# RWKV-7 mixer, r and v phases: decay factors loaded one row tile ahead, each tile's stores issued behind the next tile's products

## The chip, the cores and the metric

The kernel runs on one core of one Trainium2 chip. The metric is the device time of one execution of the whole program in microseconds; the time given is the median of several runs.

The engines are named as in the profile: PE is TensorE (matmuls; PEld is its weight load), DVE is VectorE, ACT is ScalarE, POOL is GpSimd and SP is SyncE, which issues most of the DMAs, one after the other in the order of its queue.

## The reference, cut to what matters

The model is a trunk of two layers over 1024 positions of width 1024. Layer 0 mixes tokens with a Griffin RG-LRU block, layer 1 with RWKV-7; each layer also has a cross-attention into a memory and a squared-ReLU MLP. The change touches the RWKV-7 mixer alone:

```python
def rwkv7_mixer(x, mu, w_rkv, w0, w1, w2, a0, a1, a2, g1, g2, k_k, k_a, r_k, gn_g, gn_b, w_o):
    xx = x_prev - x                       # x_prev: x shifted by one position
    r = (x + xx * mu[0]) @ w_rkv[0]
    k = (x + xx * mu[2]) @ w_rkv[1]
    v = (x + xx * mu[3]) @ w_rkv[2]
    ...                                   # decay, a, g, kk from small products
    def step(state, inp):                 # 1024 steps for each of 16 heads of 64
        r_t, w_t, k_t, v_t, a_t, b_t = inp
        sa = jnp.einsum('bhij,bhj->bhi', state, a_t)
        state = (state * w_t[:, :, None, :] + sa[..., None] * b_t[:, :, None, :]
                 + v_t[..., None] * k_t[:, :, None, :])
        y_t = jnp.einsum('bhij,bhj->bhi', state, r_t)
        return state, y_t
    _, ys = lax.scan(step, state0, seq_inputs)
    ...                                   # group norm of y, bonus term of r, k and v
    return (out * g) @ w_o
```

All values are float32. The scan is done in chunks of time, by matmuls; a small triangular system is solved in each chunk.

## The kernel before, in words

A float32 product is made of three matmuls: each operand is split into a high part, cast on ACT (L233), and a low part, subtracted on DVE (L234), and `mm3` issues high by high, high by low and low by high (L318, L319, L320). The three large products of the mixer are made one after another, k, r and v. Each is worked off in eight row tiles f of 128 channels by 1024 positions, in turns: for r the turns are [0,1], [2], [3], [4], [5] and [6,7], for v they begin with [0,1] and go on with single tiles. `fphase` makes the matmuls of one turn, 48 groups of three for each tile into one PSUM buffer `p` of 128 by 1024, of which there are two, so a tile's matmuls need the buffer that the tile two before it has left. The weights of a tile are loaded at L249 and split by L233 and L234.

In the r phase a tile is finished by `evac_r`: `early` has loaded the tile of decay factors from Pd (L1530), DVE multiplies it by the product (L1534), and SP stores the result to MVd (L1535). In the v phase `early` loads the tile of r from MVd and another from STd (L1622, L1624). `evac_v` copies the product (ACT, L1574), multiplies r by its partner (DVE, L1581) and splits this product, transposes v on TensorE (L1591), copies it to `vk` (ACT, L1592) and, behind every odd tile, stores `vk` to sv0 (L1598) and Vd (L1602). Then it makes the bonus term and the gate: matmuls against ones (L1609), DVE L1610, the three matmuls of the gate, ACT L1613 and DVE L1614, and four stores to G1d and G2d (L1617).

Beside these runs work for the triangular systems, in pieces between the turns. `gram` makes the matrices and stores them (L1426, L1427). A solve of 31 pairs of steps runs on DVE or POOL (L1447, L1449). A `merge` of solved blocks makes small matmuls (L1486, L1493) with ACT copies behind each (L1488, L1496); its operands are loaded at L1472, L1473 and L1474, and the merged block is stored at L1500. L1553 copies small tables into `db`. Near the end of the v phase the first loads of the scan are issued (L1645, L1648, L1659), and the scan itself begins with more (L1672, L1676).

What sets the order: the code is written as a list of calls, and the framework's scheduler, which simulates times of its own, puts the instructions of each engine into the one order in which that engine works them off (L1930). `self.behind()` and `self.line()` pin some of it. `depth` and `ahead` tell how many tiles ahead the weights are taken and fetched. SP waits at the head of its queue for what its next DMA needs, a DMA's source or a free buffer, and every DMA behind it waits with it.

The functions that the diff touches:

Of the kernel before, what the change touches and what calls it, by code (L numbers as in the profile page):

```python
# [1281 lines left out]
def rwkv(self, X, xt, lw_wa, lw_g, post, mid):  # L1282
    nc, I = self.nc, self.I
    mm = nc.tensor.matmul
    hgd = self.dram([128, 1024])
    Vd = self.dram([1024, 2, 512])
# [245 lines left out]
    def evac_r(f, p):  # L1532
        r = ld.pop(f)
        nc.vector.tensor_mul(r, r, p)  # L1534
        nc.sync.dma_start(MVd[:, f, 1, :], r)  # L1535

    for i, fs in enumerate([[0, 1], [2], [3], [4], [5], [6, 7]]):
        for f in fs:
            early(f)
        if i == 5:  # L1540
            self.later.append(lambda: rwkv_make_mix(self, X, 3, 0, xv[0], range(3)))
        if i in (1, 2):
            sums(5 + i)
        self.depth, self.ahead = DA if i != 4 else (DA[0], DA[1] + 1)
        self.fphase(I["b_w_rkv"][0, 0], fs, xr, evac_r, spread=i == 0)
        if i == 0:
            prep_rest(7)
        if i in (1, 2):
            gram(5 + i)
        if i == 3:  # L1550
            for par in range(2):
                for h in range(2):
                    nc.sync.dma_start(self.db.rearrange("p (f a t) -> p f a t", a=2, t=8)[hr[h], :, par],  # L1553
                                      self.d2.rearrange("p (f h t) -> p f h t", h=2, t=8)[hr[par], :, h])
        aside(len(TURNS) + i)
# [12 lines left out]
    vk = []  # L1568
    sv0 = [self.unit() for _ in range(2)]

    def evac_v(f, p):
# [15 lines left out]
        for e in range(2):  # L1587
            pt = self.bank()
            for i in range(4):
                tt = e * 4 + i  # L1590
                mm(pt[:, i * 128:i * 128 + 128], vt[:, tt * 128:tt * 128 + 128], self.center, start=True, stop=True)  # L1591
            nc.scalar.copy(vk[e].rearrange("p (t h g i) -> p t h g i", h=2, g=2, i=64)[:, :, :, f % 2, :],  # L1592
                           pt.rearrange("p (t h i) -> p t h i", h=2, i=64))
            if f % 2 and e == 0:

                for d in range(2):
                    for h in range(2):
                        nc.sync.dma_start(sv0[d][hr[1 - h], h * 512 + (f - 1) * 64:h * 512 + (f + 1) * 64],  # L1598
                                          vk[0].rearrange("p (t h i) -> p t h i", h=2, i=128)[hr[d], 0, h, :])
            if f % 2:  # L1600
                for h in range(2):
                    nc.sync.dma_start(Vd[e * 512:e * 512 + 512, h, (f - 1) * 64:(f + 1) * 64].rearrange("(t p) i -> p t i", p=128),  # L1602
                                      vk[e].rearrange("p (t h i) -> p t h i", h=2, i=128)[:, :, h, :])
        g1 = self.unit()
        for e in range(2):
            s = slice(e * 512, e * 512 + 512)
# [5 lines left out]
            self.mm3(gp, (g2[0][:, cs], g2[1][:, cs]), (hg[0][:, s], hg[1][:, s]), True, True)  # L1612
            nc.scalar.activation(g1[:, s], gp, AF.Copy, scale=self.col("gn_g", f))  # L1613
            nc.vector.scalar_tensor_tensor(vt[:, s], vt[:, s], self.col("gn_b", f), gp, ALU.add, ALU.mult)  # L1614
        for src, dst in ((g1, G1d), (vt, G2d)):
            for h in range(2):
                nc.sync.dma_start(dst[(f % 2) * 64:(f % 2) * 64 + 64, (f // 2) * 2 + h, :], src[h * 64:h * 64 + 64, :])  # L1617

    def early(f):
        cs = slice(f * 128, f * 128 + 128)  # L1620
# [142 lines left out]
    for i, fs in enumerate(turns):  # L1763
        for f in turns[i + 1] if i < 6 else []:
            early(f)
        if fs[-1] >= 5:
            self.depth, self.ahead = min(2, 7 - fs[-1]), 0
        self.fphase(I["b_w_rkv"][0, 2], fs, xv, evac_v, spread=i == 0)
        aside(len(TURNS) + 6 + i)
        if fs[-1] == LD:  # L1770
            with self.behind():
                load(0)
        if fs[-1] == 6:
            load_solved(0)
            load(1)
    with self.behind():
        load_solved(1)
    for c in range(2):
# [156 lines left out]
```

## Time and profile before

| what | value |
| --- | --- |
| runs shown | 2838.39, 2846.89, 2841.48 us; median 2841.48 |
| profiled execution | 2839.18 us, span 2837.5 us |
| mean granted TensorE clock | 0.995 |
| PE busy | 2765.8 us, 97% of the span |
| DVE, ACT, POOL busy | 1867.1, 1422.8, 907.3 us |
| r and v phases | about 1488 to 1730 us of the span |
| SP's waits for DVE L1534 at L1535, 1545 to 1700 us | 25.0 us in 4 waits, longest 12.9 |
| SP's waits for ACT L1613 at L1617, same stretch | 18.3 us in 3 waits, longest 9.8 |

A row of a timeline has the start, the duration of all its instructions together, the engine, the line and operation, output and input names, shapes and the number of instructions; in brackets stands how long the engine had been idle before it and what ended that. A row of windows gives the stretch, busy times by engine, the granted clock of TensorE, the busy share of the DMA engines and GB/s. Rows of SP are DMA issues: what they last is the time of issue, not that of the transfer.

### The profile page before, as it was taken

The page shows a single profiled execution, that of the slowest core. Times are in us where ns is not written, and L with a number is a line of the kernel's source. Part 1 is how long each engine was busy: PE and PEld are TensorE (multiplying, and loading weights), DVE is VectorE, ACT ScalarE, POOL GpSimd, SP SyncE. Part 2 cuts the span into 40 slices and gives each one's busy share as a digit, 9 for nine tenths or more (in the row PEclk, how much of TensorE's full clock was granted, in tenths as well). Part 3 has the DMA queues.
Part 4 walks back from the last instruction along what each step waited for, and adds up shares of the span by engine and source line. Part 5 has one row for each costly group of instructions (what it writes and reads, how often), then busy time and mean ns, then how long its engine had stood idle before and what let it go on. Part 6 is the DMA issues. An engine that isn't in the chain of part 4 may idle for free.

```text
span 2837.5 us, 42691 instructions
## 1 busy us (share of the span) xinstructions
PE 2765.8 (97%) x16955; PEld 2310.6 (81%) x16955; DVE 1867.1 (66%) x2017; ACT 1422.8 (50%) x2194; POOL 907.3 (32%) x962
## 2 busy tenths in 40 slices
PE   7999999999999999999999999999999999999998
PEld 6888788888888888887777777888888888888887
DVE  5477557658454577898685834785675755467778
ACT  6456355545545553346672534664563644555333
POOL 2000113014666510013088223853203376640002
PEclk9999999999999999999999999999999999999999
DMA  8212352323454554423558799962222355474453
GB/s 266 75 45 75 104 171 79 103 84 104 148 164 153 206 205 156 155 98 126 170 146 228 218 247 244 238 158 96 79 93 89 99 167 162 141 244 168 149 177 120
DMA packets 383912, 421.92 MB, mean 149 GB/s; under 512 B 91504, under 2 KB 294496, under 8 KB 383712
## 3 DMA queue, kind: packets, MB, share of 16 engines
q1 hardware_dynamic: 371680, 379.19, 44.1%
q0 software_dynamic: 11568, 39.41, 3.8%
q8 instruction: 133, 2.18, 0.3%
q14 instruction: 67, 0.55, 0.1%
q10 hardware_dynamic: 464, 0.59, 0.1%
HBM read 283.79 MB, written 134.74 MB: 148 GB/s over the span
## 4 chain that ended last, share of the span: by engine, by line
PE 44%; DVE 4%; ACT 2%; DMA 2%; issue 1%; SPq 1%; POOL 1%; DVEq 0%; POOLq 0%; ACTq 0%
PE q L318 8%; PE q L319 8%; PE q L320 8%; PE p L318 4%; PE p L320 4%; PE p L319 4%; PE q L1700 1%; DVE u L234 1%; DMA u<-d 1%; PE q L1811 1%; PE q L1823 1%; PE q L1348 1%; PE q L1724 1%; DMA u<-in_b_w_rkv 1%; PE q L1836 0%
## 5 line engine op out<-in xcount | busy, mean ns | idle before, releaser
L234 DVE TENSOR_TENSOR u<-u,u 128x1024 fp32r<-128x1024 f32 (+1 forms) x602 | 813.0, 1381 | 346.4 <-ACT u L233 331.1
L233 ACT CAST u<-u 128x1024 fp32r<-128x1024 f32 (+1 forms) x602 | 591.8, 1020 | 446.6 <-DVE u L1077 224.6
L318 PE MATMUL q<-u,u 128*128 128x512 f32 (+1 forms) x1952 | 744.7, 383 | 4.4 <-DVE u L370 2.1
L319 PE MATMUL q<-u,u 128*128 128x512 f32 (+1 forms) x1952 | 745.0, 382 | 0.0
L320 PE MATMUL q<-u,u 128*128 128x512 f32 (+1 forms) x1952 | 739.7, 382 | 0.0
L318 PE MATMUL p<-u,u 128*128 128x512 f32 (+1 forms) x1472 | 553.5, 378 | 14.5 <-ACT u L233 6.4
L319 PE MATMUL p<-u,u 128*128 128x512 f32 (+1 forms) x1472 | 552.5, 375 | 3.7 <-DVE u L234 3.5
L320 PE MATMUL p<-u,u 128*128 128x512 f32 (+1 forms) x1472 | 551.2, 375 | 4.0 <-DVE u L234 3.9
L328 POOL TENSOR_SCALAR s<-s 128x1 f32<-128x1 f32 x97 | 43.7, 451 | 1252.0 <-ACT u L326 1250.1
L318 PEld LDWEIGHTS q<-u,u 128*128 128x128 f32 x1952 | 366.9, 188 | 77.3 <-ACT u L361 1.5
L320 PEld LDWEIGHTS q<-u,u 128*128 128x128 f32 x1952 | 366.8, 188 | 71.2
L319 PEld LDWEIGHTS q<-u,u 128*128 128x128 f32 x1952 | 367.0, 188 | 70.1
L318 PEld LDWEIGHTS p<-u,u 128*128 128x128 f32 x1472 | 279.7, 190 | 67.1 <-issue 8.6
L320 PEld LDWEIGHTS p<-u,u 128*128 128x128 f32 x1472 | 279.9, 190 | 55.2 <-DVE u L234 6.2
L319 PEld LDWEIGHTS p<-u,u 128*128 128x128 f32 x1472 | 280.1, 190 | 54.4 <-DVE u L234 6.7
L443 POOL TENSOR_TENSOR u<-u,u 128x512 f32<-128x512 f32 x120 | 188.1, 1573 | 6.2 <-PE q L319 2.6
L1135 DVE TENSOR_TENSOR z<-z,q 128x512 f32<-128x512 f32 x192 | 130.7, 683 | 80.2 <-PE q L320 80.2
L320 PE MATMUL q<-z,u 128*128 128x512 f32 x320 | 124.5, 389 | 2.1 <-DVE u L234 2.1
L318 PE MATMUL q<-z,u 128*128 128x512 f32 x320 | 124.8, 390 | 0.0
L319 PE MATMUL q<-z,u 128*128 128x512 f32 x320 | 124.5, 389 | 0.0
L444 POOL TENSOR_TENSOR u<-u 128x512 f32<-128x512 f32 x40 | 68.2, 1704 | 146.2 <-DVE u L234 102.9
L1032 POOL TENSOR_TENSOR u<-u,u 128x512 f32<-128x512 f32 x32 | 46.1, 1441 | 181.7 <-ACT u L1021 172.6
(253 smaller groups left out, 3321.5 us busy)
## 6 DMA issues: line engine op xcount, KB each, us to landing
u<-d SPq DMA_DIRECT2D x194, 512.0 KB, 4.8
d<-u SPq DMA_DIRECT2D x109, 512.0 KB, 3.0
d<-u POOLq DMA_DIRECT2D x68, 512.0 KB, 3.7
d<-u SPq DMA_DIRECT2D x132, 256.0 KB, 3.4
u<-in_m_w_up SPq DMA_DIRECT2D x64, 512.0 KB, 5.4
u<-in_m_w_down SPq DMA_DIRECT2D x64, 512.0 KB, 7.3
u<-in_c_w_kv SPq DMA_DIRECT2D x32, 512.0 KB, 6.5
u<-in_b_w_rkv SPq DMA_DIRECT2D x24, 512.0 KB, 7.1
```

What stands on the lines that cost most here:

```text
L233: self.nc.scalar.copy(hv, src)
L234: (eng or self.nc.vector).tensor_tensor(lv, src, hv, ALU.subtract)
L318: mm(o, ah, bh, start=first, stop=False, **kw)
L319: mm(o, ah, bl, start=False, stop=False, **kw)
L320: mm(o, al, bh, start=False, stop=last, **kw)
L328: nc.gpsimd.tensor_scalar(v, ss, 1.0 / n, eps, ALU.mult, ALU.add)
L443: sub = lambda o, x, y: nc.gpsimd.tensor_tensor(o, x, y, ALU.subtract)
L444: nc.gpsimd.tensor_tensor(s[:, a], f1[:, a], f1[:, b], ALU.add)
L1032: tt(s1, r21, r22, ALU.add)
L1135: nc.vector.tensor_add(to_, to_, o)
L1348: mm(p, wa2[i][r, cs], hwa[j][r, s], start=n == 0, stop=n == 2)
L1700: mm(s["pv", g][h][:, q, :], s["st"][g][hr[h], q].rearrange("p w t -> p (w t)"), s["mv"][hr[h], 4 * g + q], start=True, stop=True)
```

## The change

In the r phase the decay factors of the next turn's tiles are loaded before this turn's products, so each tile's load is asked for one turn earlier; the first two tiles' loads come ahead of the loop. The stores to MVd are no longer issued in `evac_r`: they are collected in `held` and issued after the products of the next turn. What the last r turn holds is issued after the first v products.

In the v phase the stores of `vk` (sv0 and Vd) become a closure `stores_v`, one for each pair of tiles, with the stores in another order among themselves, and the four stores to G1d and G2d a closure `stores_g`. Both are held in the same way and issued after the next turn's products; the last ones come after the loop. No computation is changed, and the number of DMAs is the same.

```diff
     def evac_r(f, p):
         r = ld.pop(f)
         nc.vector.tensor_mul(r, r, p)
-        nc.sync.dma_start(MVd[:, f, 1, :], r)
-
-    for i, fs in enumerate([[0, 1], [2], [3], [4], [5], [6, 7]]):
-        for f in fs:
+        held.append(lambda: nc.sync.dma_start(MVd[:, f, 1, :], r))
+
+    held = []
+    turns = [[0, 1], [2], [3], [4], [5], [6, 7]]
+    for f in turns[0]:
+        early(f)
+    for i, fs in enumerate(turns):
+        stores, held = held, []
+        for f in turns[i + 1] if i < 5 else []:
             early(f)
...
         self.fphase(I["b_w_rkv"][0, 0], fs, xr, evac_r, spread=i == 0)
+        for st in stores:
+            st()
...
-            if f % 2 and e == 0:
-
-                for d in range(2):
+        if f % 2:
+
+            def stores_v(f=f, vk=list(vk)):
+                for e in range(2):
                     for h in range(2):
-                        nc.sync.dma_start(sv0[d][hr[1 - h], h * 512 + (f - 1) * 64:h * 512 + (f + 1) * 64],
-                                          vk[0].rearrange("p (t h i) -> p t h i", h=2, i=128)[hr[d], 0, h, :])
-            if f % 2:
-                for h in range(2):
-                    nc.sync.dma_start(Vd[e * 512:e * 512 + 512, h, (f - 1) * 64:(f + 1) * 64].rearrange("(t p) i -> p t i", p=128),
-                                      vk[e].rearrange("p (t h i) -> p t h i", h=2, i=128)[:, :, h, :])
+                        if e == 0:
+                            for d in range(2):
+                                nc.sync.dma_start(sv0[d][hr[1 - h], h * 512 + (f - 1) * 64:h * 512 + (f + 1) * 64],
+                                                  vk[0].rearrange("p (t h i) -> p t h i", h=2, i=128)[hr[d], 0, h, :])
+                        nc.sync.dma_start(Vd[e * 512:e * 512 + 512, h, (f - 1) * 64:(f + 1) * 64].rearrange("(t p) i -> p t i", p=128),
+                                          vk[e].rearrange("p (t h i) -> p t h i", h=2, i=128)[:, :, h, :])
+            held.append(stores_v)
...
-        for src, dst in ((g1, G1d), (vt, G2d)):
-            for h in range(2):
-                nc.sync.dma_start(dst[(f % 2) * 64:(f % 2) * 64 + 64, (f // 2) * 2 + h, :], src[h * 64:h * 64 + 64, :])
+
+        def stores_g():
+            for src, dst in ((g1, G1d), (vt, G2d)):
+                for h in range(2):
+                    nc.sync.dma_start(dst[(f % 2) * 64:(f % 2) * 64 + 64, (f // 2) * 2 + h, :], src[h * 64:h * 64 + 64, :])
+        held.append(stores_g)
...
+        stores, held = held, []
         if fs[-1] >= 5:
             self.depth, self.ahead = min(2, 7 - fs[-1]), 0
         self.fphase(I["b_w_rkv"][0, 2], fs, xv, evac_v, spread=i == 0)
+        for st in stores:
+            st()
...
+    for st in held:
+        st()
```

What this does to the order of the instructions, at three places. In the rows u_ names a tile in SBUF and d_ an array in HBM: d_10179 is Pd, d_10180 is MVd, d_10177 and d_10178 are G1d and G2d, d_10175 is Vd, d_10176 holds the merged blocks. The number behind u_ differs a little between the two programs.

First, SP in the r phase. Before, at the load of tile 4's decay factors:

```order
L1472 DMA u_12384<-d_10184 32x16x32 x4
L1473 DMA u_12386<-d_10185 32x16x32
L1474 DMA u_12386<-d_10182 32x512
L1530 DMA u_12395<-d_10179 128x1024
L249 DMA u_12397<-in_b_w_rkv 128x8x128
L1473 DMA u_12546<-d_10185 32x16x32
```

Now, where this load (here u_12258) stands:

```order
L1382 DMA d_10180<-u_11810 128x1024
L1535 DMA d_10180<-u_11945 128x1024
L1530 DMA u_12258<-d_10179 128x1024
L1426 DMA d_10183<-u_12142 32x8x32 x2
L1427 DMA d_10182<-u_12142 256x1x32
```

The load of tile 4 has moved from behind the merge's loads to a place ahead of the gram's stores, where tile 3's load stood before; where it was, tile 5's load stands now, and the store ahead of it is that of tile 2.

Second, ACT at the merges of the r phase (L1488 and L1496 are the merges' copies, L233 the casts of weights). Before:

```order
L233 CAST u_12399<-u_12260 128x1024
L1488 COPY u_12386<-q_12474 32x512 x2
L233 CAST u_12559<-u_12397 128x1024
L1496 COPY u_12384<-q_12509 32x16x32 x2
L1488 COPY u_12546<-q_12632 32x512 x2
L233 CAST u_12718<-u_12557 128x1024
```

Now:

```order
L233 CAST u_12400<-u_12261 128x1024
L233 CAST u_12562<-u_12398 128x1024
L1488 COPY u_12387<-q_12475 32x512 x2
L233 CAST u_12717<-u_12560 128x1024
L1496 COPY u_12385<-q_12510 32x16x32 x2
L1488 COPY u_12547<-q_12635 32x512 x2
```

The cast of tile 7's weights of r now stands ahead of the first merge's first copy, and that of the first weights of v ahead of its second.

Third, SP in the v phase. Before, ahead of the last weights of v (u_13741):

```order
L1602 DMA d_10175<-u_13412 128x4x128 x2
L1617 DMA d_10177<-u_13619 64x1024 x2
L1617 DMA d_10178<-u_13592 64x1024 x2
L1645 DMA u_13727<-d_10181 128x8x64 x2
L1645 DMA u_13730<-d_10181 128x8x64 x2
L1648 DMA z_13726<-d_10180 128x8x128 x2
L1622 DMA u_13736<-d_10180 128x1024
L1624 DMA u_13737<-d_10181 64x1024 x2
L249 DMA u_13741<-in_b_w_rkv 128x8x128
```

Now, at the loads of tile 4 (u_13528 and u_13529) and on to the weights behind them:

```order
L1500 DMA d_10176<-u_12958 128x1024
L1608 DMA u_13032<-u_13158 64x128
L1608 DMA u_13033<-u_13158 64x128
...
L1634 DMA u_13528<-d_10180 128x1024
L1636 DMA u_13529<-d_10181 64x1024 x2
L249 DMA u_13533<-in_b_w_rkv 128x8x128
```

And at the last weights of v (u_13729):

```order
L1610 DMA d_10175<-u_13396 128x4x128
L1657 DMA u_13715<-d_10181 128x8x64 x2
L1657 DMA u_13718<-d_10181 128x8x64 x2
L1634 DMA u_13724<-d_10180 128x1024
L1636 DMA u_13725<-d_10181 64x1024 x2
L249 DMA u_13729<-in_b_w_rkv 128x8x128
L1610 DMA d_10175<-u_13396 128x4x128
L1628 DMA d_10177<-u_13607 64x1024 x2
```

The last weights have lost tile 3's stores to G1d and G2d (L1617, now L1628), which come behind them, and the two L1648 loads, which come a turn earlier. Tile 4's loads, which stood directly behind merge 2's store, now stand behind merge 3's (L1500 u_12958) and four stores to sv0 (L1598, now L1608). DVE, PE and ACT keep their order but for a few neighbours; outside the two phases nothing moves.

## The prediction

> **What bounds the kernel now.** I read the page first, then TensorE's own timeline across the r and v phases, looking only at its idle times, and then followed each idle time back through ACT, DVE and SP. The page:
>
> ```profile
> PE 2765.8 (97%) x16955; PEld 2310.6 (81%) x16955; DVE 1867.1 (66%) x2017; ACT 1422.8 (50%) x2194; POOL 907.3 (32%) x962
> ```
>
> TensorE is busy for 97% of the span, so only its few idle times, and the slower clock behind them, can be won. The ones that this change can reach, on TensorE's timeline (start, duration, what ran, the idle time ahead of it and what ended it):
>
> ```profile
> 1560.77 0.47 PE L318 MATMUL p<-u,u 128*128 128x512 f32 x1 [3.78 <-DVE u L1534]
> 1598.63 0.73 PE L318 MATMUL p<-u,u 128*128 128x512 f32 x2 [1.97 <-ACT u L233]
> 1697.55 0.22 PE L1493 MATMUL q<-u,u 32*32 32x32 f32 x2 [3.37 <-issue]
> 1698.11 1.10 PE L1493 MATMUL q<-u,u 32*32 32x32 f32 x48 [0.34 <-ACT u L1488]
> ```
>
> Call them gap A (3.78 us, r phase), the mix gap (1.97, while the inputs of the v products are made) and gap B (3.37 + 0.34 = 3.71, v phase). What follows a gap stands in the windows view (after the stretch and its length the busy times of PE, PEld, DVE, ACT and POOL; then granted clock, DMA share, GB/s):
>
> ```profile
> 1561.00:1565.00 4.00, 4.00 (x44) 2.87 (x45) 3.83 (x7) 3.40 (x6) 3.69 (x5) 0.65 0.80 199
> 1565.00:1570.00 5.00, 5.00 (x58) 4.28 (x53) 4.79 (x8) 1.29 (x3) 4.37 (x9) 0.94 0.80 194
> 1599.00:1604.00 5.00, 4.47 (x13) 3.28 (x12) 5.00 (x9) 5.00 (x10) 0.00 (x0) 0.66 1.01 328
> 1698.00:1702.00 4.00, 3.89 (x73) 3.83 (x74) 2.66 (x3) 3.39 (x6) 0.57 (x1) 0.59 0.87 255
> ```
>
> Lost to the clock: after A (1 - 0.65) x 4 + (1 - 0.94) x 5 = 1.7 us; after the mix gap 0.34 x 5 = 1.7; after B 0.41 x 4 = 1.6. So A costs 5.5 us in all, the mix gap 3.7 and B 5.3.
>
> **The change part by part: gap A.** No instruction is added; DMAs change place in SP's queue. Behind gap A stand these rows of DVE, ACT and SP:
>
> ```profile
> 1547.33 1.22 DVE L1534 TENSOR_TENSOR u<-u,p 128x1024 f32<-128x1024 f32 x1 [6.16 <-DMA u<-d]
> 1559.41 1.21 DVE L1534 TENSOR_TENSOR u<-u,p 128x1024 f32<-128x1024 f32 x1
> 1555.66 0.72 DVE L1447 TENSOR_TENSOR w<-u,u 128x175 f32<-128x175 f32 x1
> 1557.06 1.66 DVE L234 TENSOR_TENSOR u<-u,u 128x1024 fp32r<-128x1024 f32 x1
> 1549.38 1.05 ACT L233 CAST u<-u 128x1024 fp32r<-128x1024 f32 x1 [1.41 <-DMA u<-in_b_w_rkv]
> 1543.17 0.36 SPq L1530 DMA_DIRECT2D u<-d  x1
> 1511.75 0.42 SPq L1530 DMA_DIRECT2D u<-d  x1
> ```
>
> The load of tile 4's decay factors went out only at 1543.17, behind the gram's stores, the copies into db and the merge's loads. Its product held up DVE for 6.16 us; the solve's steps and tile 5's product (ended 1560.62) queue behind it there, and tile 7's matmuls need the PSUM buffer that tile 5's product frees. In the change tile 4's load takes the place of tile 3's, issued at 1511.75, and tile 5's takes 1543.17. With the wait out, what comes last ahead of tile 5's product on DVE is the split of tile 7's weights, whose cast ends at 1549.38 + 1.05 = 1550.4; then 1.66 for the split, 0.72 for the one solve step behind it and 1.21 for the product make 1554.0 (an estimate; the steps before them have the time for it). TensorE stopped at 1560.77 - 3.78 = 1557.0: 3.0 us of room, and the whole 5.5 us of A are won. If the load came as late as now, nothing would be.
>
> The new order puts something in its place, on ACT:
>
> ```profile
> 1553.19 1.16 ACT L1496 COPY u<-q 32x512 f32<-32x512 f32 x2 [2.75 <-PE q L1493]
> 1554.37 1.18 ACT L1488 COPY u<-q 32x512 f32<-32x512 f32 x2
> 1559.97 1.05 ACT L233 CAST u<-u 128x1024 fp32r<-128x1024 f32 x1 [4.41 <-DMA u<-in_b_w_rkv]
> 1564.11 1.79 PE L1493 MATMUL q<-u,u 32*32 32x32 f32 x64
> 1552.81 2.96 SPq L249 DMA_DIRECT2D u<-in_b_w_rkv  x2
> DMA to landing us min/median/max: 4.0/7.1/14.5
> ```
>
> The cast at 1559.97 (weights of v's first tile) stood behind the copies of the merge; now it stands ahead of L1496 of merge 0 and L1488 of merge 1. TensorE wants that L1488 for its L1493, at 1564.11 now, without gap A at 1560.3. The weights, issued at 1552.81, go out at about 1551.4, an estimate, since SP no longer waits for tile 4's late product; with the median of L249's landings (7.1, the last row) they are there at 1558.5, and after 1.05 + 1.16 + 1.18 us L1488 ends at 1561.9: 1.6 us of new stall. At the fastest landing (4.0) it is done by 1558.8, no stall; with the weights as late as before (1559.97) it ends at 1563.4, a stall of 3.1. A stall of that size can also slow the clock:
>
> ```profile
> 1497.41 0.77 PE L318 MATMUL p<-u,u 128*128 128x512 f32 x1 [1.29 <-DVE u L1534]
> 1490.00:1500.00 10.00, 8.71 (x67) 7.44 (x67) 10.00 (x11) 6.30 (x6) 9.37 (x9) 0.87 0.86 267
> ```
>
> The 1.29 us gap has 0.13 x 10 = 1.3 us of lost clock around it. I take half, 0.7, since the stall may be split in shorter ones. So A: 5.5 - 1.6 - 0.7 = **3.2 us** won; at best 5.5, at worst 5.5 - 3.1 - 1.7 = 0.7.
>
> The Trainium skill ("TensorE: Matmul & The Clock Gate", Part 1: The HAM clock gate) states that the clock goes to half only after an idle window of some 3.4 us. By that rule the 1.6 us stall would cost no clock and the whole would be 0.7 us better. This trace goes against it: the 1.97 us gap is followed by a clock of 0.66.
>
> **The mix gap.** It hangs on casts and splits in DVE's and ACT's queues, in which the solve's steps are interleaved.
>
> ```profile
> 1581.63 1.21 DVE L234 TENSOR_TENSOR u<-u,u 128x1024 fp32r<-128x1024 f32 x1
> ```
>
> DVE's head start is cut back where it must wait for tile 6's matmuls. What stays is this split, 1.21 us, which then runs ahead of tile 6's product instead of behind it. I take **1.2 us**; it is 0 if ACT sets the pace (busy 5.00 of 5.00 us in the window at 1599), and at most the whole 3.7.
>
> **Gap B.** Rows of ACT and SP, and one of the chain of waits (start, length, what):
>
> ```profile
> 1695.22 1.04 ACT L233 CAST u<-u 128x1024 fp32r<-128x1024 f32 x1 [11.31 <-DMA u<-in_b_w_rkv]
> 1661.57 2.80 SPq L1602 DMA_DIRECT2D d<-u  x4
> 1665.49 3.02 SPq L1617 DMA_DIRECT2D d<-u  x4
> 1668.57 4.51 SPq L1645 DMA_DIRECT2D u<-d  x4
> 1673.12 3.36 SPq L1648 DMA_DIRECT2D z<-d  x2
> 1680.66 14.46 DMA u<-in_b_w_rkv
> ```
>
> The last weights of v were issued at 1680.66 and needed 14.46 us. ACT waited 11.31 us for them, with L1613 and the merge's L1488 queued behind the cast, and TensorE for those. The change takes out ahead of this load tile 3's four L1617 stores (3.02) with the wait before them (1665.49 - 1664.37 = 1.1) and the two L1648 loads (3.36, now a turn earlier): 7.5 us. Issued at 1673.2 it lands at 1687.6, and TensorE stopped at 1694.2: over 5 us of room for the cast. **5.3 us** are won; nothing, if landing is not earlier (below).
>
> In exchange tile 4's early loads stand behind merge 3's store, which waits for ACT, and behind four held L1598 stores:
>
> ```profile
> 1640.93 1.16 ACT L1496 COPY u<-q 32x512 f32<-32x512 f32 x2 [3.18 <-PE q L1493]
> 1637.24 0.86 SPq L1500 DMA_DIRECT2D d<-u  x1
> 1658.95 2.58 SPq L1598 DMA_DIRECT2D u<-u  x4
> 1638.62 0.61 SPq L1622 DMA_DIRECT2D u<-d  x1
> 1651.09 1.28 DVE L1581 SCALAR_TENSOR_TENSOR u<-u,colt,u 128x1024 f32<-128x1024 f32 x1 [0.68 <-DMA u<-d]
> 1654.69 1.23 DVE L234 TENSOR_TENSOR u<-u,u 128x1024 fp32r<-128x1024 f32 x1 [2.32 <-ACT u L233]
> 1658.81 0.71 PE L1609 MATMUL q<-u,ones_r 128*128 128x512 f32 x2
> DMA to landing us min/median/max: 6.8/10.2/15.4
> ```
>
> In the times of this trace the load, now at 1638.62, goes out at 1640.93 + 1.16 + 0.86 + 2.58 = 1645.5. It feeds L1581, which has L234 behind it on DVE, and L1609 on TensorE waits for that; so it must be there by 1658.81 - 1.23 - 1.28 = 1656.3, after 10.8 us. The median landing of L1622 (10.2, last row) leaves 0.6 us; this tile's own load took 12.5 (1638.62 to 1651.09), 1.7 too long; the slowest (15.4) 4.6 too long, and with 1.7 of clock 6.3. I take **1.0 us** lost, between the first two.
>
> Stores sent later cost nothing that I can find: G1d, G2d and Vd are read in the scan, several turns on, and the last ones keep their order ahead of the scan's loads. A tile buffer held one turn longer could make a later load wait; no idle time in the rows names a buffer, so I take 0.
>
> **Sum:** 3.2 + 1.2 + 5.3 - 1.0 = 8.7 us. The profiled execution took 2839.18 us (span 2837.5), so it would take 2830.5; the median of the runs shown is 2841.48, 2.3 above it and inside their spread of 8.5 (2838.39 to 2846.89), which gives **2832.8 us**. With every term at its best end: 5.5 + 3.7 + 5.3 = 14.5, or 2827.0; at its worst: 0.7 + 0 + 5.3 - 6.3 = -0.3, or 2841.8.
>
> **The rivals.** *The waits only move*: the weights come late in both places, ACT stalls at A and DVE at tile 4's loads; the gain is 0 to 5.5 us, at its middle 2838.7. For it: ACT already waited 4.41 us for just these weights; against it: both bounds take the late end at once.
>
> *B is set by bandwidth, not by the issue.* The window before B:
>
> ```profile
> 1680.00:1690.00 10.00, 10.00 (x112) 8.44 (x111) 1.44 (x2) 1.86 (x3) 0.66 (x1) 1.00 1.12 232
> ```
>
> With a DMA share above 1 until 1690 the load could land as late as now, and the earlier issue would buy a longer landing. Then A and the mix alone remain: 3.2 + 1.2 - 1.0 = 3.4, or 2838.1. Against it: 3.02 us worth of stores now come after the load, not before it. The Trainium skill ("DMA: Bandwidth & Descriptors", Issuing engines are not separate DMA queues) has all queues share the same 16 DMA engines, so that only time at the issue is saved; the window agrees as far as it goes.
>
> *Held stores block the loads*, the slower case: SP takes its queue in order, and from tile 3 on every early load of v stands behind stores that may still wait for ACT. It decides from a landing of over 10.8 us. If it strikes at the full price in three tiles, 3 x 6.3 = 18.9 against 9.7 won is 9.2 lost: 2850.7. For it: 12.5 us is what tile 4's load took; against it: most held stores are of a tile already finished.
>
> *The change does not do what it says*, if the order of the queues were as before; the listed order speaks against that. 2841.5.
>
> **How the numbers follow.** Forecast (gain 5.5 to 14.5) 0.55; waits move 0.21; bandwidth 0.10; held stores block 0.11; no change of order 0.03. About 0.3%, 8.5 us, is what a measurement of this kernel can tell from no change: faster means under 2833.0. Within the forecast case, taken evenly over its range, two thirds lie over 8.5 and, since I shaded A, the mix and tile 4 downwards, I give three quarters: 0.41 faster. The rest of it and the three middle cases are the same: 0.48; slower 0.11. The range goes from 2825 (best end and some spread) to 2846 (worst end and the like), and leaves out chiefly the slower case.
>
> **What would show it.** Right: L1534 of tile 4 with no wait for a DMA and no gap of over 1 us on TensorE before tile 7's matmuls; the last weights issued some 7 us earlier against TensorE and no idle time at L1493 in the v phase. Wrong: a new gap over 3 us at merge 1's L1493 or at L1609, with a slow clock behind it; ACT still waiting for weights at B; SP idle for long at a held store while a load stands behind it.

## The result

The change runs in 2830.72 us (median of 6 runs, 2827.03 to 2832.8) against 2839.67 us of the kernel before (6 runs, 2837.45 to 2846.89): 9.0 us less, a ratio of 0.9967 with a 95% interval of 0.9956 to 0.9978. The same kernel measured again in a later session gave 0.9965 (0.9953 to 0.9977). The forecast was 2832.8 us, 8.7 less than the 2841.48 of the three runs shown before. The profiled execution took 2832.8 us, 6.4 less than the one of before.

The page of the change, first part:

```profile
PE 2767.1 (98%) x16955; PEld 2313.6 (82%) x16955; DVE 1866.0 (66%) x2017; ACT 1422.9 (50%) x2194; POOL 910.1 (32%) x962
```

TensorE's timeline of the change in the r and v phases, the row behind its longest idle time, and the first and the last tile's transposes of v (L1598 is before's L1591):

```profile
1565.59 0.31 PE L1493 MATMUL q<-u,u 32*32 32x32 f32 x2 [4.63 <-DMA d<-u]
1608.68 2.05 PE L1598 MATMUL q<-center,u 128*128 128x128 f32 x16 [0.42 <-ACT u L1581]
1720.12 2.05 PE L1598 MATMUL q<-center,u 128*128 128x128 f32 x16 [1.15 <-ACT u L1581]
```

Gap A (3.78 us) is gone, and so are the mix gap (1.97) and its smaller neighbours: between 1566 and 1608 us no idle time over 0.25 us is left. Gap B (3.71 us at L1493 in the v phase) is gone too. One new gap stands there, 4.63 us at merge 1's L1493. It is the stall that the forecast had put at 1.6 us, in its place, and larger. The forecast had also named "a new gap over 3 us at merge 1's L1493" with a slow clock behind it as a sign that it was wrong; in this execution that sign is there. What the clock did behind it (windows of the change, columns as before):

```profile
1566.00:1570.00 4.00, 4.00 (x67) 3.21 (x68) 3.93 (x6) 3.64 (x6) 3.61 (x6) 0.50 0.85 198
1570.00:1575.00 5.00, 5.00 (x17) 3.98 (x16) 5.00 (x7) 3.50 (x6) 4.45 (x8) 0.68 0.20 80
1690.00:1710.00 20.00, 20.00 (x216) 16.68 (x215) 5.29 (x6) 7.40 (x12) 4.32 (x6) 1.00 0.68 218
```

Behind the new gap 0.50 x 4 + 0.32 x 5 = 3.6 us are lost. Where gap B was, TensorE now works the full 20 us at clock 1.00.

To compare stages I use three instructions that both programs have: a matmul just ahead of the r phase (L319), and the first and the last tile's transposes of v. Of before:

```profile
1482.09 0.50 PE L319 MATMUL p<-u,u 128*128 128x512 f32 x1 [0.40 <-DVE u L234]
1612.58 2.05 PE L1591 MATMUL q<-center,u 128*128 128x128 f32 x16 [0.42 <-ACT u L1574]
1728.85 2.05 PE L1591 MATMUL q<-center,u 128*128 128x128 f32 x16 [1.10 <-ACT u L1574]
```

Of the change, with the rows of 1608.68 and 1720.12 above:

```profile
1480.48 0.50 PE L319 MATMUL p<-u,u 128*128 128x512 f32 x1 [0.33 <-DVE u L234]
```

The r stage (first to second) took 130.5 us before and 128.2 now, the v stage (second to third) 116.3 and 111.4: 2.3 and 4.8 us less, 7.1 in all. Outside these stages the two executions differ by 0.7 us the other way: the change's was 1.6 us shorter ahead of the r stage and 2.3 longer behind the v stage. When the change was measured again, the part behind the v stage was 0.7 us shorter than in before, so I do not count this as an effect of the change.

Behind the r stage, rows of DVE, SP and ACT of the change:

```profile
1535.35 1.22 DVE L1534 TENSOR_TENSOR u<-u,p 128x1024 f32<-128x1024 f32 x1 [6.92 <-PE p L320]
1551.99 1.21 DVE L1534 TENSOR_TENSOR u<-u,p 128x1024 f32<-128x1024 f32 x1
1548.25 4.31 SPq L1472 DMA_DIRECT2D u<-d  x4
1552.69 1.98 SPq L1530 DMA_DIRECT2D u<-d  x1
1554.77 1.93 SPq L249 DMA_DIRECT2D u<-in_b_w_rkv  x2
1562.70 1.05 ACT L233 CAST u<-u 128x1024 fp32r<-128x1024 f32 x1 [11.38 <-DMA u<-in_b_w_rkv]
1563.77 1.16 ACT L1496 COPY u<-q 32x512 f32<-32x512 f32 x2
1564.96 1.18 ACT L1488 COPY u<-q 32x512 f32<-32x512 f32 x2
```

Tile 4's product (1535.35) now waits for TensorE, not for its load, and tile 5's ends at 1553.2, where 1554.0 was forecast. (Times of the two executions are compared as they stand; at merge 0's first matmul, L1486 at 1543.15 in before and at 1542.56 in the change, they lie 0.6 us apart.) The first weights of v went out at 1554.77, not at 1551.4: SP spent 4.31 us on merge 1's four loads and 1.98 on tile 7's decay factors just ahead of them, where before it had spent 1.97 and 0.49. Part of this is a wait for a store to land (SP's waits of the change from 1545 to 1565 us: total, times, longest):

```profile
SPq L1472 <- DMA d<-u: 2.2, 1, 2.2
```

The store is a held one, to MVd: SP issued it at 1543.47, then seven more DMAs, and the eighth, merge 1's third load, only at 1551.59, when the store had landed after 8.1 us. The weights were cast at 1562.70, 7.9 us after their issue (7.1 was taken), and L1496 and L1488 stood behind the cast on ACT, in the order that the forecast had read. TensorE could go on only when the first half of that L1488 was done. (The row of the gap names a DMA as its end; by these times it was this copy, as the row of the change measured again, `[1.99 <-ACT u L1488]`, says outright.)

Behind the v stage, rows of SP, DVE, PE and ACT of the change:

```profile
1642.27 0.53 SPq L1634 DMA_DIRECT2D u<-d  x1
1649.93 1.28 DVE L1588 SCALAR_TENSOR_TENSOR u<-u,colt,u 128x1024 f32<-128x1024 f32 x1
1654.53 0.48 PE L1618 MATMUL q<-u,ones_r 128*128 128x512 f32 x1
1668.24 0.54 SPq L249 DMA_DIRECT2D u<-in_b_w_rkv  x1
1677.22 1.05 ACT L233 CAST u<-u 128x1024 fp32r<-128x1024 f32 x1 [0.68 <-DMA u<-in_b_w_rkv]
```

Tile 4's load went out at 1642.27, 33.6 us after the first tile's transposes; before it was 1638.62 - 1612.58 = 26.0. So it is 7.6 us later, and 6.9 was forecast (1645.5 for 1638.62). It was there in time all the same, within 7.7 us where the forecast had 10.2 to 12.5: L1588 did not wait, nor did TensorE at L1618. The last weights went out 59.6 us after the first tile's transposes instead of 68.1, 8.5 us earlier (7.5 forecast), and ACT waited 0.68 us for them instead of 11.31; from issue to cast they took 9.0 us instead of 14.6.

### The profile page after: what moved, and what is told of

It is laid out like the page before. It is cut to its first block, busy times and chain, and to the rows that moved or that the text cites. A ratio compares the mean times of both kernels' runs of the same rounds, so it can differ in the third digit from the quotient of the medians.

```text
span 2831.1 us, 42698 instructions
## 1 busy us (share of the span) xinstructions
PE 2767.1 (98%) x16955; PEld 2313.6 (82%) x16955; DVE 1866.0 (66%) x2017; ACT 1422.9 (50%) x2194; POOL 910.1 (32%) x962
## 4 chain that ended last, share of the span: by engine, by line
PE 89%; DVE 4%; ACT 2%; issue 2%; POOL 1%; DMA 1%; SPq 1%; ACTq 0%; DVEq 0%; POOLq 0%
PE q L318 17%; PE q L320 17%; PE q L319 17%; PE p L318 10%; PE p L320 9%; PE p L319 9%; PE q L1712 1%; DMA u<-d 1%; DVE u L234 1%; PE q L1840 1%; PE q L389 1%; PE q L1828 1%; PE q L1348 1%; ACT u L326 1%; PE q L1598 1%
## 5 line engine op out<-in xcount | busy, mean ns | idle before, releaser
L233 ACT CAST u<-u 128x1024 fp32r<-128x1024 f32 (+1 forms) x602 | 591.9, 1020 | 448.6 <-DVE u L1077 224.6
L319 PE MATMUL q<-u,u 128*128 128x512 f32 (+1 forms) x1952 | 746.6, 383 | 0.0
L319 PE MATMUL p<-u,u 128*128 128x512 f32 (+1 forms) x1472 | 553.5, 376 | 2.5 <-DVE u L234 2.4
L319 PEld LDWEIGHTS q<-u,u 128*128 128x128 f32 x1952 | 367.7, 188 | 70.1
L319 PEld LDWEIGHTS p<-u,u 128*128 128x128 f32 x1472 | 280.7, 191 | 52.5 <-DVE u L234 5.1
L319 PE MATMUL q<-z,u 128*128 128x512 f32 x320 | 124.6, 389 | 0.0
```

The source lines that it names most:

```text
L233: self.nc.scalar.copy(hv, src)
L319: mm(o, ah, bl, start=False, stop=False, **kw)
```

## The experiments

All times are ratios to the kernel before in the same session, with 95% intervals; 0.001 is 2.8 us. Kernels of different sessions are compared by these ratios. The stages are those above, from one profiled execution each. The clock alone makes the r stage of one execution up to some 3 us longer than that of another (last section), so small differences between single r stages mean nothing.

| kernel | ratio | interval | r stage, us | v stage, us |
| --- | --- | --- | --- | --- |
| before | 1 | | 130.5 | 116.3 |
| the change | 0.9967 | 0.9956 to 0.9978 | 128.2 | 111.4 |
| the change again | 0.9965 | 0.9953 to 0.9977 | 127.7 | 111.4 |
| r part alone | 0.9997 | 0.9986 to 1.0008 | 126.1 | 116.7 |
| v part alone | 0.9982 | 0.9970 to 0.9994 | 132.9 | 110.8 |
| v part, stores to G1d and G2d only | 0.9981 | 0.9970 to 0.9993 | 129.3 | 111.4 |
| change, r stores at once | 0.9978 | 0.9967 to 0.9988 | 129.0 | 111.3 |
| change, r loads as before | 0.9977 | 0.9968 to 0.9986 | 127.3 | 112.1 |
| change, v's first split pinned | 0.9976 | 0.9966 to 0.9985 | 123.8 | 117.0 |
| change, tiles 6 and 7 loaded in their own turn | 0.9975 | 0.9966 to 0.9983 | 128.7 | 111.4 |
| change, more clearing on DVE | 0.9992 | 0.9983 to 1.0002 | 128.4 | 115.3 |
| change, clearing on ACT | 1.0025 | 1.0013 to 1.0036 | 139.3 | 118.2 |
| change, fourth solve on POOL | 1.0094 | 1.0079 to 1.0108 | 153.8 | 119.3 |
| the same and tiles 6 and 7 in their own turn | 1.0087 | 1.0074 to 1.0100 | 154.9 | 121.5 |

### The two parts apart

The r part alone: the change with the `evac_v` of before, whose stores go out at once (the lines that put the stores of vk back into `evac_v` are left out here).

```diff
-            held.append(stores_v)
...
-        held.append(stores_g)
+        for src, dst in ((g1, G1d), (vt, G2d)):
+            for h in range(2):
+                nc.sync.dma_start(dst[(f % 2) * 64:(f % 2) * 64 + 64, (f // 2) * 2 + h, :], src[h * 64:h * 64 + 64, :])
```

> The r phase alone as in the change; the v phase stores at once as before (only the last held r stores come behind v's first products). My theory (two independent gains): gap A and the mix gaps go, the new stall of 4.6 us at the L1493 of merge 1 is there as in the change's trace, gap B (3.7 us at L1493 in the v phase) stays: about 3.5 us less than before, that is the 3.3 that the change's trace gained on before's between 1543 and 1612 us. Rival (the gain of the v phase comes from the shift of TensorE in the r phase and not from its own stores): gap B goes here too and the whole 9 us are gained.

It gave 0.9997 (0.9986 to 1.0008). TensorE's timeline of this kernel:

```profile
1560.28 0.24 PE L1493 MATMUL q<-u,u 32*32 32x32 f32 x2 [2.58 <-ACT u L1488]
1691.12 0.22 PE L1493 MATMUL q<-u,u 32*32 32x32 f32 x2 [2.29 <-issue]
1691.67 1.50 PE L1493 MATMUL q<-u,u 32*32 32x32 f32 x62 [0.34 <-ACT u L1488]
```

Gap B is there (2.63 us), so the v phase's gain does not come from the shift of the r phase: the rival falls. The new stall is there with 2.58 us. The 3.5 us expected are near the edge of what the interval allows (at most 4.0). In the profiled execution the r stage was 4.4 us shorter than in before, but by the 12 runs the kernel gained 0.9: one execution does not tell.

The v part alone: the r phase of before.

```diff
-        held.append(lambda: nc.sync.dma_start(MVd[:, f, 1, :], r))
+        nc.sync.dma_start(MVd[:, f, 1, :], r)
...
-        for f in turns[i + 1] if i < 5 else []:
+        for f in fs:
             early(f)
```

> The v phase alone as in the change; the r phase loads and stores as before. My theory: gap A (3.8 us) and the mix gaps stay, the last weights of v go out some 7 us earlier and gap B goes: about 5.3 us less than before (3.7 of gap and 1.6 of clock). Rival (B is set by the bandwidth, or by the shift of TensorE in the r phase): gap B stays or comes back as an equal wait, and the time is before's within 1.5 us.

It gave 0.9982 (0.9970 to 0.9994), 5.1 us where 5.3 were expected. TensorE's timeline of this kernel still has the gaps of the r phase, and none at L1493 of the v phase:

```profile
1562.92 0.77 PE L318 MATMUL p<-u,u 128*128 128x512 f32 x1 [3.79 <-DVE u L1534]
1601.66 0.73 PE L318 MATMUL p<-u,u 128*128 128x512 f32 x2 [1.97 <-ACT u L233]
```

That B was set by bandwidth is refuted: with the load issued earlier the wait went, and it did not come back as a longer landing (from issue to cast 8.6 us here, 14.6 before).

The change itself in the session of later runs:

> The change itself, on the chip of the three kernels below, so that they can be compared with it. Both phases' gains together were 0.9967 of before; the r part alone gave 0.9997 and the v part alone 0.9982 in another session. If the parts add up, the change gives about 0.998 of before here (5 to 6 us); if the r part is worth more beside the v part, it gives 0.9967 again (9 us).

It gave 0.9965 again. The parts alone add up to 6.0 us, the change has 9.4 and 9.9. Beside the v part (0.9982 and 0.9981 in two kernels without the change's r phase) the r part is worth 0.0016, 4.4 us, with about 3.4 to either side; alone it is worth 0.9 us with 3.1 to either side. The stage table, with three executions on each side, has 127.3 us for the change's r phase (126.1 to 128.2) and 130.9 for that of before (129.3 to 132.9): 3.6 us, of which the clock's own scatter may be a good part. So the r part is worth some 1 to 5 us; whether it gains more beside the v part than alone is not settled by these runs.

### What in the v part counts

Only the stores to G1d and G2d are held, those of vk go out at once, the r phase is that of before (its lines are left out here).

```diff
-            held.append(stores_v)
+            stores_v()
```

> The v phase with only the stores to G1d and G2d held; the stores of vk at once, the r phase as before. My theory: it is these stores (3.0 us and the wait for ACT ahead of them) that stood ahead of the last weights, so gap B goes and the whole gain of the v part is there, 0.998 of before (5 us). Rival (the gain comes from the earlier loads of z, which the held vk stores let through): gap B shrinks by half at most, 0.9995.

It gave 0.9981, the whole gain of the v part. In its profile the last weights go out 61.4 us after the first tile's transposes (68.1 before), and the gap at L1493 is gone. The held stores of vk bring nothing that can be seen here. The order of the queue differs from before in one thing more, though: the two loads of z, 3.36 us of issue that stood ahead of the last weights (L1648 at 1673.12), go out a turn earlier in this kernel too (at 1651.10). How the gain divides between the four stores and these two loads was not separated.

### What in the r part counts

The change, but the r stores go out at once:

```diff
-        held.append(lambda: nc.sync.dma_start(MVd[:, f, 1, :], r))
+        nc.sync.dma_start(MVd[:, f, 1, :], r)
```

> The change, but the r stores to MVd go out at once; their loads stay one tile ahead, the v phase is the change's. My theory (in the r phase only the earlier loads count: no store to MVd was waited for): 0.9966 of before, as the change, within 0.001. Rival (the held stores give SP the room): 0.998, as the v part alone.

And the change, but the decay factors are loaded in their own turn:

```diff
-    for f in turns[0]:
-        early(f)
...
-        for f in turns[i + 1] if i < 5 else []:
+        for f in fs:
             early(f)
```

> The change, but the decay factors are loaded in their own turn as before; the r stores are held, the v phase is the change's. My theory: gap A stays for the most part, since tile 4's load stands behind the merge's loads again, and the time is that of the v part alone, 0.998 of before, 4 us above the change. Rival (the r part is worth nothing, as its run alone, 0.9997, would have it): 0.9966, as the change.

They gave 0.9978 and 0.9977, both nearer to the v part alone than to the change, but with intervals that touch both. The first was not expected by my theory, by which only the loads count; the second was. TensorE's timeline, first of the kernel with r stores at once:

```profile
1561.51 0.24 PE L1493 MATMUL q<-u,u 32*32 32x32 f32 x2 [2.34 <-ACT u L1488]
1596.51 0.73 PE L318 MATMUL p<-u,u 128*128 128x512 f32 x2 [1.84 <-ACT u L233]
```

then of the kernel with the loads as before:

```profile
1556.99 0.47 PE L318 MATMUL p<-u,u 128*128 128x512 f32 x1 [1.88 <-DVE u L1534]
1581.16 0.76 PE L318 MATMUL p<-u,u 128*128 128x512 f32 x1 [5.08 <-DVE u L1534]
```

With the loads ahead gap A goes and the stall at merge 1 comes; without them half of gap A stays and 5.08 us at v's first product come. In both the rest of the stage differs as well (1.84 us of the mix gap stay in the first). Which of the two edits brings the r part's few microseconds stays open.

### The new stall

The change with v's first weights split in a block that is pinned behind merge 1, which puts their cast behind L1488 and L1496 of merge 1 on ACT:

```diff
+        if i == 5:
+            with self.behind():
+                self.fetch(self.taken)
         self.fphase(I["b_w_rkv"][0, 0], fs, xr, evac_r, spread=i == 0)
```

> The change, with the first weights of v fetched and split in a block of its own that is pinned behind merge 1 in the order of each engine: on ACT the cast of these weights now stands behind L1488 and L1496 of merge 1 instead of ahead of them; DMAs of the r phase keep their order up to there. My theory (the new stall is made by ACT's order alone): the 4.6 us stall at L1493 and the slow clock behind it (0.50 for 4 us and 0.68 for 5, some 3.6 us) go, and no other takes their place, since v's first product comes 15 us later: 5 to 8 us less than the change, 2823 to 2826. Rival (the late weights hold up the following work in any order, so that the waits move on to the mix): the gaps at 1590 to 1600 us come back, and the time is within 2 us of the change's 2830.7.

The stall at L1493 went, so it was ACT's order, with the late weights, that made it, and the r stage fell to 123.8 us, the shortest of all. But the time did not fall: 0.9976. TensorE's and DVE's timelines of this kernel show where it went:

```profile
1618.93 2.05 PE L1601 MATMUL q<-center,u 128*128 128x128 f32 x8 [4.43 <-DVE u L1622]
1616.90 1.28 DVE L1591 SCALAR_TENSOR_TENSOR u<-u,colt,u 128x1024 f32<-128x1024 f32 x1 [2.57 <-DMA u<-d]
```

In the order that the scheduler made for this kernel, DVE multiplies the third v tile (L1591, waiting 2.57 us for its load) ahead of the first tiles' L1622, and TensorE waits 4.43 us for that. So the rival was right that the wait moves on, though not in the place that it named.

The change with tiles 6 and 7 loaded in their own turn:

```diff
-        for f in turns[i + 1] if i < 5 else []:
+        for f in turns[i + 1] if i < 4 else []:
             early(f)
+        if i == 5:
+            for f in turns[5]:
+                early(f)
```

> The change, but the decay factors of tiles 6 and 7 are loaded in their own turn, as before, so that these two loads stand behind the first weights of v in SP's queue and not ahead of them. My theory: the weights were late because SP issued them at 1554.8 and not at 1551.4 as I had put it, 2.4 us of that being these two loads; the stall at merge 1's L1493 falls from 4.6 to about 2.2 us and the time by 2.4 to 3.5, to about 2827.5. Rival (the issue is held by the limit on outstanding DMAs, and the landing by the DMA engines): the stall stays within 0.7 us of 4.6 and the time within 1.5 us of 2830.7.

Here v's first weights went out at 1548.31 and the stall at L1493 went altogether, more than the 2.4 us expected. The time is 0.9975, no better than the change. Rows of TensorE, SP and DVE of this kernel:

```profile
1560.31 1.20 PE L1493 MATMUL q<-u,u 32*32 32x32 f32 x64
1583.67 0.77 PE L318 MATMUL p<-u,u 128*128 128x512 f32 x1 [6.76 <-ACT u L1459]
1548.31 0.42 SPq L249 DMA_DIRECT2D u<-in_b_w_rkv  x1
1582.31 1.22 DVE L1534 TENSOR_TENSOR u<-u,p 128x1024 f32<-128x1024 f32 x1
```

v's first product waits 6.76 us, until the product of tile 6 on DVE (1582.31 + 1.22) has freed its PSUM buffer. The releaser that the row names, L1459, is not what it waited for by these times; DVE's product ends 0.14 us before TensorE goes on. DVE comes to that product 1.8 us later than in before (1580.50), although TensorE was there earlier: it would have begun at 1576.9, in before at 1581.3.

### Is DVE the pace of the stage?

That was my second theory: between tile 5's product and the v products DVE, with POOL beside it, sets the time, and any stall removed from TensorE comes back as a wait for DVE. More work on DVE, each merge's clearing of its block four times instead of once:

```diff
-        (nc.vector if f < 4 else nc.gpsimd).memset(XT, 0.0)
+        for _ in range(4 if f < 4 else 1): (nc.vector if f < 4 else nc.gpsimd).memset(XT, 0.0)
```

> The change, with each merge's clearing of its block on DVE made four times instead of once (merges 0 to 3: twelve extra clearings of 0.91 us, 10.9 us of DVE work, eight to nine us of it between 1550 and 1610 us). Theory (DVE paces the stage between tile 5's product and the v products): the time rises by 6 to 11 us over the change. Rival (DVE has room there, what remains are DMA waits): by less than 2 us.

It gave 0.9992 (0.9983 to 1.0002), 7 us above the change for 10.9 us of work, inside the 6 to 11 expected. The r stage did not grow (128.4 us); the v stage did, by 4 us. In this profile the fourth solve's steps on DVE, which end at 1605.7 in the change, run on to 1629.4, and DVE is busy for 16.7 of the 17 us from 1605 on. So DVE has no room for this work, but the place where it costs is not the one that the theory named: it is behind the stage, in the first v tiles.

Less work on DVE, the same clearings on ACT:

```diff
-        (nc.vector if f < 4 else nc.gpsimd).memset(XT, 0.0)
+        nc.scalar.activation(XT.rearrange("p (a b) -> p a b", b=128), self.ones.unsqueeze(1).broadcast_to([128, 8, 128]), AF.Copy, scale=0.0) if f < 4 else nc.gpsimd.memset(XT, 0.0)
```

> The change, with the clearings of merges 0 to 3 on ACT (one instruction of some 1 us each) instead of DVE: 0.91 us less on DVE for each merge, three of them between 1550 and 1610 us. Theory (DVE paces): 1 to 2.7 us below the change, 0.9960. Rival (DVE has room; or ACT, which has the late casts in its queue, is the one that decides): the same as the change or up to 3 us above it.

It gave 1.0025, some 17 us above the change, more than either expected. The theory cannot be read from it, since another wait took over. Rows of SP and TensorE of this kernel:

```profile
1558.38 0.40 SPq L249 DMA_DIRECT2D u<-in_b_w_rkv  x1
1573.59 0.33 SPq L1460 DMA_DIRECT2D d<-u  x1
1574.01 0.39 SPq L249 DMA_DIRECT2D u<-in_b_w_rkv  x1
1581.56 0.31 PE L1486 MATMUL q<-u 32*32 32x32 f32 x2 [6.72 <-DMA u<-d]
```

The scheduler put the third solve's store (L1460) ahead of weights of v and of merge 2's loads. SP waited at it from 1558.8 to 1573.6, until POOL had solved, and all that was behind it was late.

The fourth solve on POOL, behind the third, instead of on DVE:

```diff
-SE = [lambda nc: nc.gpsimd] * 3 + [lambda nc: nc.vector]
+SE = [lambda nc: nc.gpsimd] * 4
...
-            if q == 3:
-                self.between.append(lambda s=s: one(s))
-            else:
-                one(s)
+            one(s)
```

> The change, with the fourth triangular solve (31 pairs of steps, some 35 us of DVE time between 1540 and 1608 us) on POOL behind the third, instead of on DVE between the matmuls. My theory now (DVE, with POOL beside it, paces the stage from 1550 to 1610 us, so that what the r part removes comes back as another wait there): with this work off DVE the waits for DVE go, those of merge 1 for the weights' cast stay (4.6 us in the change's trace), POOL's solves run faster than 43.7 us without DVE's steps beside them. Time 2 us either side of the change; DVE busy from 1545 to 1610 falls from 55.7 to some 30 us. Rival (DVE's load does not matter, waits are set by DMAs): the same gaps, and the time within 1 us of the change's.

The same with tiles 6 and 7 loaded in their own turn:

> The kernel whose tiles 6 and 7 load their decay factors in their own turn (no stall at merge 1, but a 6.8 us stall at v's first product, for L1534 of tile 6, behind DVE's queue), with the fourth solve on POOL as well. My theory (DVE paces): the 6.8 us gap goes with DVE's load and the merge 1 stall stays away, so the stage from 1545 to 1610 has less than 3 us of idle TensorE and the time is 5 to 8 us below the change: about 0.994 of before. Rival (the wait goes to yet another place, ACT or SP): at most 2 us below the change.

They gave 1.0094 and 1.0087, 27 and 25 us above before, and neither expectation held. Rows of SP, of SP's waits between 1540 and 1640 us, and of ACT, all of the first:

```profile
1550.80 0.53 SPq L1532 DMA_DIRECT2D d<-u  x1
1572.73 0.32 SPq L1457 DMA_DIRECT2D d<-u  x1
SPq L1457 <- POOL u L1449: 47.0, 2, 25.6
1578.38 1.04 ACT L233 CAST u<-u 128x1024 fp32r<-128x1024 f32 x1 [17.34 <-DMA u<-in_b_w_rkv]
```

It is the same thing again: a solve's store (L1457 here) at the head of SP's queue, 21 us with nothing issued, and v's weights behind it, for which ACT waited 17.34 us. A second wait of 25.6 us follows at the next solve's store; in the other kernel two such waits take 53.8 us. These three kernels did not test what they were made for. What they show is the mechanism of the forecast's slower rival at work: with a store that waits for POOL ahead of v's weights they took 17, 37 and 35 us more than the change. How much of the last two is due to POOL's longer chain of solves was not separated.

So that DVE sets the pace is borne out by one of the four runs made for it and is not shown. No kernel tried is faster than the change.

## Why the prediction was right

**The sum.** 8.7 us were forecast, 9.0 measured, and the sign and the range hold. That the two lie so close is in part luck: the interval of the 9.0 goes from 6.2 to 12.5 us, in the change's two profiled executions the two stages became 7.1 and 7.7 us shorter, and the parts of the sum were not equally good.

**Gap B: right.** 5.3 us were forecast from its idle time and its clock; the v part alone, for which the sum has 5.3 - 1.0 = 4.3, gave 5.1 (1.7 to 8.5), and the v stage is 4.8 us shorter in the change. The rows that carried it were read rightly: the stores to G1d and G2d and the loads of z ahead of the last weights, as the kernel that holds only these stores shows.

**Tile 4's loads: right in the delay, too careful in the price.** The load went out 7.6 us later, as forecast within 0.7, and it cost nothing where 1.0 us was taken. The term lay between 0 and 6.3, and 0 was its better end.

**Gap A: right in mechanism, the new stall mis-sized.** The load one tile ahead did take DVE's 6.16 us wait away, with tile 5's product within 0.8 us of the forecast, and gap A with it. The term that failed is the stall at merge 1's L1493 with its clock: 1.6 + 0.7 us were taken, 3.1 + 1.7 was the worst end. The change's profile has 4.63 + 3.6. The change again has 1.99, and its windows

```profile
1567.00:1571.00 4.00, 3.92 (x69) 3.28 (x70) 3.90 (x6) 3.95 (x7) 3.67 (x5) 0.60 0.96 193
1571.00:1576.00 5.00, 5.00 (x16) 3.96 (x15) 5.00 (x7) 2.58 (x5) 4.53 (x7) 0.64 0.49 173
```

0.40 x 4 + 0.36 x 5 = 3.4 us of clock. The stall's idle part is thus 2 to 4.6 us (2.58 and 2.34 in two other kernels with this order), and the clock behind it about 3.5, twice the worst end. Two steps failed. The issue of v's first weights was put at 1551.4 from the removed wait alone; the merge's four loads and the tile's load ahead of it were taken to cost SP what they had before (1.97 and 0.49 us), and they took 4.31 and 1.98, 3.8 us more; the delay was 3.4. And the clock was priced by a shorter gap near 1497 us, at half of its price.

**The mix gap: mis-sized the other way.** 1.2 us were taken; in the change's profile all of it went, 1.97 us with 1.7 of clock and the smaller gaps beside it (0.56, 0.42, 0.44, 0.53 and 0.53 us in before). In the change again 0.89 + 0.53 are left. It may be that DVE and ACT went on and caught up while TensorE stood still at merge 1; this is not shown. The kernel with r stores at once has a stall of 2.34 us there and keeps 1.84 us of the mix gap, and the kernel with v's first split pinned has no stall there and only 0.72 + 0.53 us of idle time in the mix. The two errors cancel in part: for the r stage 3.2 + 1.2 = 4.4 us were forecast, and it became 2.3 and 2.8 shorter in the change's two profiles, 3.6 in the mean of the stage table. That they would cancel was not foreseen, so this is luck: the two terms were priced as if they were independent.

**The rivals.** That the waits only move fits the r phase taken by itself: both attempts to take out the new stall brought another wait within 60 us, and the r part alone is worth 0.9 us with 3.1 to either side. It is wrong for the v phase. The bandwidth rival fell with the v part alone. The slower rival did not strike in the change. SP did wait at merge 3's store ahead of tile 4's load (SP's waits in the v phase of the change: total, times, longest),

```profile
SPq L1500 <- ACT u L1496: 7.1, 1, 7.1
```

but the load had the room.

## What to carry to other kernels

Look for a store that waits for its producer ahead of a load in an in-order DMA queue: with the four stores and two other loads out of the load's way, 5 us came free here, and three kernels in which a waiting store got ahead of a load were 17 to 37 us slower than the change. Gap B, which hung on one late load, was won whole; the gaps of the r stage, where DVE is busy for nine tenths of the time (53.4 of 60 us from 1550 on in the change) and ACT, SP and POOL feed one another, were not, since the wait came back at another engine. So price the gaps of such a stage together and not one by one. Read the new order of every queue, not only of the one edited: the stall that took gap A's place was to be seen in ACT's order before any run.

## What the runs showed of the hardware

What a gap costs in clock is not set by its length. Behind 1.99 us of idle time 3.4 us were lost, behind 4.63 us 3.6, but behind gap A of before, 3.78 us, only 1.7. Windows laid over the slow stretch alone show what such a price is made of. Behind gap A of before, and behind the 1.99 us of the change again:

```profile
1562.20:1565.50 3.30, 3.30 (x57) 2.39 (x57) 3.13 (x6) 2.93 (x5) 2.91 (x6) 0.50 0.76 157
1567.80:1574.60 6.80, 6.80 (x74) 5.67 (x73) 6.73 (x9) 4.41 (x7) 6.17 (x9) 0.50 0.81 199
```

In both the clock is at half throughout, for some 3.4 us in the one and twice that in the other, so the one lost 1.7 us and the other 3.4. The losses read above are all near one such stretch (1.7, 1.7 and 1.6 us in before) or two (3.4 and 3.6). Even one and the same gap differs between executions. The gap at the first r tiles' products near 1496 and 1500 us, 1.18 us long in both, in the kernel with only the stores to G1d and G2d held and in the change again (windows right behind it, in this order):

```profile
1495.60:1502.90 7.30, 7.26 (x32) 6.04 (x33) 7.22 (x7) 0.00 (x0) 6.91 (x6) 1.00 0.91 300
```

```profile
1499.60:1502.90 3.30, 3.30 (x8) 2.62 (x9) 3.30 (x5) 0.00 (x0) 3.06 (x4) 0.50 0.98 331
```

No clock lost in the one, 0.5 x 3.3 = 1.7 us in the other; in the change's first profile, at 1.19 us of idle time, the clock is 0.50 from 1494.7 to 1501.4 us, in which TensorE works for 5.8, so 2.9 are lost. Nor does it take one long gap: in the kernel with v's first split pinned the longest idle time in the five microseconds ahead of the next window is 0.57 us, amid the small matmuls of the merges (32x32). What makes the clock fall there is not shown.

```profile
1558.40:1561.70 3.30, 3.30 (x8) 2.65 (x9) 3.16 (x5) 1.44 (x3) 2.99 (x5) 0.50 0.75 235
```

The Trainium skill ("TensorE: Matmul & The Clock Gate", Part 1: The HAM clock gate) says that the window in which activity is counted runs freely, so that the same kernel can fall differently on it; the rows of the 1.18 us gap agree with that. Its figure of some 3.4 us of idle time before the clock falls does not agree with them: 1.18 us were enough once, and 1.99 us in the change again.
